# Hybrid encoder block on one core: values' stores on another queue, key halves written by the engines, other pages behind the last gates

## Chip, cores and metric

One Trainium2 chip, one core of it. The metric is the device time of one execution of the whole program in microseconds; lower is better. All arithmetic is fp32: an fp32 product is made of three matmuls on a rounded part ("high", written by ScalarE as a copy to the matmul's fp32r type) and the rest of the number ("low", written by VectorE as a subtraction).

## Reference

One layer of a streaming encoder on x (512 tokens, width 2048):

```python
h = rms_norm(x, norm_mix_w)
q_a, k_a, v_a, q_g, k_g, v_g, r_g, gate_lr = split_cols(h @ w_in, IN_SPLITS)
y_a = chunked_band_attention(q_a, k_a, v_a, att_rel_bias)       # 16 heads of 64, chunks of 64 frames, 8 chunks back
o_g = gated_linear_attention(q_g, k_g, v_g, log_a)              # 4 heads, keys 128, values 256 wide
y_g = rms_norm(o_g, gla_norm_w) * silu(r_g)
x = x + concat(y_a, y_g) @ w_out
h = rms_norm(x, norm_ffn_w)
u_gate, u_val = split(causal_depthwise_conv(h @ w_ffn_up, w_ffn_conv, b_ffn_conv))
x = x + (gelu(u_gate) * u_val) @ w_ffn_down
g = sigmoid(rms_norm(x, norm_ple_w) @ w_ple_gate)
x = x + g * (p @ w_ple_proj)                                    # per-layer embedding p, 256 wide
return rms_norm(x, final_norm_w)
```

In the attention, scores are `q·k / 8 + bias`, a softmax over the keys of the band, and the weighted sum of the values.

## The kernel before

Activations are kept transposed: 128 rows of features by 512 tokens. The program runs in this order: the values of the gated linear attention, its four heads, the values of the softmax attention (`values_a(0)`, then `values_a(1)`, each for 8 of the 16 heads), then a list of *steps*.

**Values.** `values_a(c)` calls `vproj`, which accumulates four PSUM tiles `ps[t]` (one for 128 tokens), and ScalarE copies them, scaled, into four half pages (`vstage`). Four DMAs on SyncE's queue then store them to the scratch tensor `vad` in DRAM (L1018). Each attention unit later loads its 128 columns back as `va` (L710). Before `vproj` of `c = 1` copies its results, it calls `operands_left`, which issues eight loads of operands of the input stage (`in_N`, `in_T`, `in_R`, L337).

**Steps.** The other matrix products are done in the form of a seven-product block scheme. A *unit* is a pair of 128-row output blocks; it takes seven steps P1, P2, P6, P5, P7, P3, P4, each of 24 matmuls of 128x256 for a full-length product. The stages, in order: `pp` (embedding products, units 0 and 1, one step `PP` each), `in` (12 units: 0 to 7 queries and keys of one pair of heads each, 8 to 11 the gates `r_g`), `pp` (units 2 and 3), `wo` (output projection, 8 units, its first two interleaved step by step), `up`, three `dn` stages, `pg`.

The loop over the steps writes the order of the engines by hand: for step *i* it emits ScalarE's high part and VectorE's low part of the weights of step *i*+2, the step's matmuls, and what an *agenda* holds for this step, sorted by a small number (below 2 ahead of the product, from 2 on behind it); then `collect` takes the finished product from PSUM into the unit's page `unit.o`, named `u` in the profile. For VectorE, ScalarE and TensorE the program order is kept in this part; DMAs on the queues of SyncE, ScalarE and GpSimd are placed by the compiler's scheduler.

**Pages.** 128x1024 fp32 buffers have fixed tags, and `page(ring, name)` hands them out in turn from a ring of tags. At first ring `c` is only (`c0`) and ring `u` is (`u0`, `u1`); after the last attention unit (`attention_done`) `c` is (`c1`, `c2`, `c0`) and `u` is (`u2`, `u3`, `u0`, `u1`). A page that is handed out again is written only when its earlier readers, stores among them, are done.

After the switch ring `c` gives, in this order: `on` of gates 1 and 2 (`after_gates`, the attention's result that a gate multiplies), `pT` (the embedding's input), `on` of gate 3, two `pp_o` pages of embedding unit 2, two of unit 3, then `xs` of the `wo` units. Ring `u` gives `u2` and `u3` to gates 2 and 3, and `u0`, `u1` to the first two units of `wo`.

**Embedding.** `embedding(unit)` makes four products into PSUM (`pp`), ScalarE copies them into two `pp_o` pages, and after each second copy a DMA on ScalarE's queue stores the page to `ppd` (L687).

**Attention.** `attend(unit)` returns agenda items relative to the end of the unit's products, so that the attention of a pair of heads runs beside the products of the next unit. For each of the two heads `s` of a pair, the query page holds the high part of Q in one half of the partitions and the low part in the other, and the key pages `Kh` and `Kl` must hold the same 64 rows twice, once in each half, so that one matmul gives high plus low. `high` (ScalarE, second step) writes Q's high part and one half of `Kh`; `low` (VectorE, third step) writes Q's low part into the other half and one half of `Kl`; `double` (third step) copies each half to the other with four DMAs on GpSimd's queue. `scores` (from the fifth step on) multiplies into `psc`, `soft`, `normal`, `turn`, `evict` and `values` follow.

GpSimd's queue also carries the weight loads that add in place (`accum_op`, L404), which make the sums of weight blocks that the scheme needs.

Of the kernel before, what the change touches and what calls it, by code (L numbers as in the profile page):

```python
# [8 lines left out]
F32 = mybir.dt.float32  # L9
F32R = mybir.dt.float32r  # L10
I32 = mybir.dt.int32
AF = mybir.ActivationFunctionType
ALU = mybir.AluOpType

P = 128
# [26 lines left out]
def encoder_block(ctx: ExitStack, tc: tile.TileContext, A, out):  # L42
    nc = tc.nc
# [4 lines left out]
    pg = ctx.enter_context(tc.tile_pool(name="pages", bufs=1))  # L48
# [21 lines left out]
    vec, act, ten = InOrder(nc.vector), InOrder(nc.scalar), InOrder(nc.tensor)  # L70
# [26 lines left out]
    def page(ring, name, dt=F32, shape=(P, 1024)):  # L97
        tags = rings[ring]
        i = counts.get(ring, 0)
        counts[ring] = i + 1  # L100
        tag = tags[i % len(tags)]
        return page_pool(tag).tile(list(shape), dt, tag=tag, name=name)
# [562 lines left out]
    vad, ond = scratch("vad", (8, P, TT, P)), scratch("ond", (4, P, 2, T))  # L665
    ps_, early = [], []
# [6 lines left out]
    def embedding(unit):  # L673

        hi, lo = unit.w["PP"]
        for i in range(4):
            if i % 2 == 0:
                o = (early[0].tile([P, 1024], F32, tag="pp_o", name="pp_o", bufs=4) if unit.u < 2 else page("c", "pp_o"))
                o = o.rearrange("p (s t) -> p s t", s=2)
            pp = psum_aux("pp")  # L680
            for k in range(2):
                w = slice((i * 2 + k) * P, (i * 2 + k + 1) * P)
                product3(pp, hi[:, w], lo[:, w], ps_[0][:, k], k == 0, k == 1)
            act.activation(o[:, i % 2, :], pp, AF.Copy)
            if i % 2:
                m = 4 * unit.u + i - 1
                nc.scalar.dma_start(ppd[m % 8:m % 8 + 2, m // 8].rearrange("m p t -> p m t"), o)  # L687
# [6 lines left out]
    def attend(unit):  # L694
        b, M = unit.u, {}
        o = unit.o

        def tile_(name, cols, dt=F32, tag=None, bufs=1):
            return att[0].tile([P, cols], dt, tag=tag or name, name=name, bufs=bufs)

        def load_e():
            for s in range(2):
                nc.sync.dma_start(bias[:, s, :], A["bias"][2 * b + s])

        def mask():
            vec.memset(bias[0:64, :, T - CHUNK:T], NEG)

        def load_v():
            M["V"] = tile_("va", T).rearrange("p (k v) -> p k v", k=TT)
            nc.sync.dma_start(M["V"], vad[b])  # L710

        def high():
            for n in ("Q", "Kh", "Kl"):
                for s in range(2):
                    M[n, s] = tile_(f"{n}{s}", T, F32R)
            for s in range(2):
                a = slice(s * 64, s * 64 + 64)
                act.activation(M["Q", s][a], o[a, 0, :], AF.Copy, scale=0.125)
                act.activation(M["Kh", s][a], o[a, 1, :], AF.Copy)

        def low():
            for s in range(2):
                a, z = slice(s * 64, s * 64 + 64), slice(64 - s * 64, 128 - s * 64)
                vec.scalar_tensor_tensor(M["Q", s][z], o[a, 0, :], 0.125, M["Q", s][a].bitcast(F32), ALU.mult, ALU.subtract)
                vec.tensor_tensor(M["Kl", s][a], o[a, 1, :], M["Kh", s][a].bitcast(F32), ALU.subtract)

        def double():
            for s in range(2):
                a, z = slice(s * 64, s * 64 + 64), slice(64 - s * 64, 128 - s * 64)
                for n in ("Kh", "Kl"):  # L730
                    nc.gpsimd.dma_start(M[n, s][z], M[n, s][a])

        def scores(h):
            for s in range(2):
                psc = M["psc", s, h] = psum_aux("psc")
                for i, qt in enumerate(TILES[h]):
                    w = slice(256 * i, 256 * i + max(P * (qt + 1), 256))
                    nn = w.stop - w.start
                    ql = M["Q", s][:, qt * P:(qt + 1) * P]
                    ten.matmul(psc[:, w], ql, M["Kh", s][:, :nn], start=True, stop=False)  # L740
                    ten.matmul(psc[:, w], ql, M["Kl", s][:, :nn], start=False, stop=True)

        def soft(h):
            t, at = tile_("sc", 1024, bufs=2), 0
            for s in range(2):
                for i, qt in enumerate(TILES[h]):
                    n = P * (qt + 1)
                    sc = M["sc", s, qt] = t[:, at:at + n]
                    mx = M["mx", s, qt] = tile_("mx", 4, bufs=8)
                    at += n  # L750
                    vec.tensor_tensor_reduce(sc, M["psc", s, h][:, 256 * i:256 * i + n], bias[:, s, T - n:T], 1.0, -3.0e38,
                                             ALU.add, ALU.max, mx[:, 0:1])
                    vec.tensor_scalar(mx[:, 1:2], mx[:, 0:1], -1.0, None, ALU.mult)
                    act.activation(sc, sc, AF.Exp, bias=mx[:, 1:2], accum_out=mx[:, 2:3])

        def normal(h):
            for s in range(2):
                for qt in TILES[h]:
                    sc, mx = M["sc", s, qt], M["mx", s, qt]
                    vec.reciprocal(mx[:, 3:4], mx[:, 2:3])  # L760
                    vec.tensor_scalar(sc, sc, mx[:, 3:4], None, ALU.mult)

        def turn(h):
            for s in range(2):
                ptr = M["ptr", s] = psum_aux("ptr")
                for i, qt in enumerate(TILES[h]):
                    for kt in range(qt + 1):
                        ten.transpose(ptr[:, (2 * i + kt) * P:(2 * i + kt + 1) * P], M["sc", s, qt][:, kt * P:(kt + 1) * P], ident)

        def evict(h):  # L770
            n = 3 * P if h else T
            M["PT"] = tile_("PT", 2 * T).rearrange("p (s t) -> p s t", s=2)
            for s in range(2):
                act.activation(M["PT"][:, s, :n], M["ptr", s][:, :n], AF.Copy)

        def values(h):
            if h == 0:
                M["y"] = pp_.tile([P, T], F32, tag="b3", name="py")
            for i, qt in enumerate(TILES[h]):
                for kt in range(qt + 1):  # L780
                    for s in range(2):
                        o = (2 * i + kt) * P
                        ten.matmul(M["y"][s * 64:(s + 1) * 64, qt * P:(qt + 1) * P], M["V"][:, kt, s * 64:(s + 1) * 64],
                                   M["PT"][:, s, o:o + P], start=kt == 0, stop=kt == qt)

        def result():
            if b % 2 == 0:
                ypair[:] = [page("c", "yp").rearrange("p (s t) -> p s t", s=2)]
            act.activation(ypair[0][:, b % 2, :], M["y"], AF.Copy)

        items = [(2, 0, load_e), (2, 2, high), (3, 1, low), (3, 3, double), (4, 1, mask), (5, 0, load_v), (11, 1, result)]
        if b % 2:
            items.append((12, 1, lambda: store_pair(mixd, b // 2, ypair[0][:, 0, :], ypair[0][:, 1, :])))
        for h in range(3):
            items += [(t + h, k, lambda f=f, h=h: f(h)) for t, k, f in (
                (5, 6, scores), (6, 1, soft), (7, 1, normal), (7, 5, turn), (8, 1, evict), (8, 4, values))]
        return items
# [54 lines left out]
    agenda = [[] for _ in range(len(steps) + 60)]  # L852
    now = [0]
    for a, b in zip(stages[3:], stages[4:]):
        i0 = base[a.units[-1]]
# [12 lines left out]
    i0 = base[front.units[-1]]  # L868
# [12 lines left out]
    def embedding_load(raw):  # L881
        nc.sync.dma_start(raw.rearrange("p (k t) -> p k t", k=2), A["p"].rearrange("k p t -> p k t"))
        return raw
# [4 lines left out]
        vec.tensor_tensor(t[:, 1, :], raw, t[:, 0, :].bitcast(F32), ALU.subtract)  # L888

    raws = {}  # L890
    agenda[i0 + 2].append((0, lambda: raws.update(p=embedding_load(page("c", "pT")))))
    agenda[i0 + 6].append((1, lambda: embedding_split(raws["p"], xtile("N1", 1, "ps"))))

    def attention_done():
# [116 lines left out]
    def values_a(c, between=None, then=None):  # L1011
        def place(t):
            vstage[c, t] = xslot(4 * c + t, "va")
            return vstage[c, t]

        vproj(A["w_v_a"], c, place, between=between, then=then)
        for t in range(TT):
            nc.sync.dma_start(vad[4 * c:4 * c + 4, :, t].rearrange("b p v -> p b v"),  # L1018
                              vstage[c, t].rearrange("p (b v) -> p b v", b=4))

    shim = ctx.enter_context(tc.tile_pool(name="shim", bufs=1, side="right")).tile([P, 240], F32, tag="shim", name="shim")
# [213 lines left out]
    for i, (unit, prod) in enumerate(steps[:-4]):  # L1235
# [19 lines left out]
        if i - len(steps) in EARLY:  # L1255
            p, op, g = EARLY[i - len(steps)]
# [160 lines left out]
```

## Time and profile before

| | |
|---|---|
| median of 3 runs | 2329.81 us (2325.82 to 2332.3) |
| profiled execution, device time | 2329.97 us |
| its span, first to last instruction | 2328.3 us |
| mean granted TensorE clock | 0.99 |
| busy in the span: PE, DVE, ACT, POOL | 2273.8, 1879.8, 1287.6, 161.1 us |
| DMA | 520.84 MB, mean 224 GB/s |
| 300 to 317 us | end of the second values product |
| 317 to 329 us | first embedding products |
| 329 to 650 us | input stage, from 372 us on with the attention beside it |
| 650 to 663 us | second embedding products |
| from 663 us | output projection, then the feed-forward stages |

Rows of a timeline give start, length, engine, line, operation, `out<-in` by the program's names, the count of merged instructions, and in brackets how long the engine had idled before and what ended that. "ACTq" and "SPq" are the queues of ScalarE and SyncE when they issue a DMA. Rows of a table by stretches give the stretch, its length, the busy time and instruction count of PE, PEld, DVE, ACT and POOL, the granted clock, the share of the DMA engines and GB/s. Most code of the steps goes through one helper and so has line L64; the tile names tell the operations apart.

### The profile page before, as it was taken

How to read it: one execution, taken by the hardware profiler on the slowest of the kernel's cores; microseconds unless marked ns; L12 is line 12 of the kernel's file. 1: busy time of each engine (PE TensorE's matmuls, PEld its weight loads, DVE VectorE, ACT ScalarE, POOL GpSimd, SP SyncE). 2: the span in 40 equal slices, each digit the busy share in tenths (PEclk: the TensorE clock that was granted, in tenths of full speed). 3: DMA queues.
4: the chain of work that ended last, by engine and by line, in shares of the span. 5: the costliest groups of instructions: out<-in, count | busy, mean ns of one | idle time of the engine just before them, and what ended most of it. 6: DMA issues, size and time to landing. Idle time of an engine off the chain costs nothing.

```text
span 2328.3 us, 44943 instructions
## 1 busy us (share of the span) xinstructions
PE 2273.8 (98%) x17980; PEld 2190.4 (94%) x17980; DVE 1879.8 (81%) x2557; ACT 1287.6 (55%) x1878; POOL 161.1 (7%) x212
## 2 busy tenths in 40 slices
PE   9999999999999999999999999999999999999996
PEld 8878879999989999999999999999999999999995
DVE  6556357888788898998888888888898787898987
ACT  6344355666565565555555555555564554656655
POOL 0000001111000010000000100000000100001000
PEclk9999999999999999999999999999999999999998
DMA  6622577777897987788777777777866967879894
GB/s 217 195 77 89 174 265 182 194 197 198 262 303 242 298 237 210 209 221 219 215 210 218 208 219 209 210 218 210 254 211 228 317 223 237 274 254 329 264 293 158
DMA packets 198033, 520.84 MB, mean 224 GB/s; under 512 B 21408, under 2 KB 72864, under 8 KB 197824
## 3 DMA queue, kind: packets, MB, share of 16 engines
q1 hardware_dynamic: 167296, 422.54, 52.2%
q0 software_dynamic: 26176, 89.14, 21.4%
q10 hardware_dynamic: 4352, 6.29, 0.7%
q8 instruction: 141, 2.31, 0.4%
q14 instruction: 68, 0.56, 0.1%
HBM read 435.05 MB, written 76.55 MB: 220 GB/s over the span
## 4 chain that ended last, share of the span: by engine, by line
PE 82%; DVE 7%; DMA 6%; ACT 3%; issue 2%; SPq 0%; POOL 0%; ACTq 0%; DVEq 0%; POOLq 0%
PE accA L64 38%; PE accC L64 19%; PE accB L64 10%; PE v L249 3%; PE v L251 2%; PE v L250 2%; DVE wl L64 2%; DMA Kl<-Kl 1%; DMA s<-in_w_blk 1%; DVE s L64 1%; DMA s<-in_w_dn 1%; DVE u L64 1%; PE pk L133 1%; PE pk L132 1%; PE pk L134 1%
## 5 line engine op out<-in xcount | busy, mean ns | idle before, releaser
L64 DVE TENSOR_TENSOR wl<-s,wh 128x1024 fp32r<-128x1024 f32 (+1 forms) x365 | 437.8, 1200 | 67.4 <-ACT wh L64 66.5
L64 DVE TENSOR_TENSOR wl<-l,wh 128x1024 fp32r<-128x1024 f32 (+1 forms) x308 | 368.5, 1196 | 73.3 <-ACT wh L64 72.6
L64 ACT ACTIVATE wh<-l 128x1024 fp32r<-128x1024 f32 (+1 forms) x308 | 319.2, 1037 | 182.5 <-PE accC L64 120.0
L64 ACT ACTIVATE wh<-s 128x1024 fp32r<-128x1024 f32 (+1 forms) x365 | 378.0, 1037 | 36.0 <-DVE s L64 16.6
L64 ACT ACTIVATE u<-accA 128x256 f32<-128x256 f32 x290 | 110.0, 379 | 378.0 <-PE accA L64 377.5
L64 DVE TENSOR_TENSOR s<-s,l 128x1024 f32<-128x1024 f32 (+1 forms) x192 | 229.7, 1196 | 8.7 <-DMA s<-in_w_blk 8.7
L64 PE MATMUL accA<-up_T,wh 128*128 128x256 f32 x1408 | 178.7, 279 | 0.1
L64 PEld LDWEIGHTS accA<-up_T,wh 128*128 128x128 f32 x1408 | 170.5, 188 | 0.3 <-ACT wh L64 0.3
L64 DVE SCALAR_TENSOR_TENSOR cv<-u,cw,cv 128x511 f32<-128x511 f32 (+1 forms) x176 | 131.6, 748 | 3.1
L404 POOL DMA_DIRECT2D s<-in_w_up x88 | 75.1, 853 | 790.3 <-DMA s<-in_w_up 363.3
L249 PE MATMUL v<-wv_h,h 128*128 128x512 f32 x256 | 100.2, 391 | 0.6 <-ACT h L154 0.6
L250 PE MATMUL v<-wv_l,h 128*128 128x512 f32 x256 | 100.4, 392 | 0.0
L251 PE MATMUL v<-wv_h,h 128*128 128x512 f32 x256 | 99.9, 391 | 0.0
L64 PE MATMUL accA<-up_T,wl 128*128 128x256 f32 x704 | 96.3, 279 | 0.0
L64 PE MATMUL accA<-dn_T,wh 128*128 128x256 f32 x704 | 91.3, 282 | 4.2 <-ACT wh L64 4.2
L64 ACT ACTIVATE u<-accC 128x256 f32<-128x256 f32 x94 | 36.0, 383 | 106.6 <-PE accC L64 106.5
L64 PE MATMUL accB<-up_R,wh 128*128 128x256 f32 x704 | 90.4, 280 | 2.0 <-DVE up_R L64 1.3
L64 PEld LDWEIGHTS accA<-dn_T,wh 128*128 128x128 f32 x704 | 86.5, 190 | 4.8 <-ACT wh L64 4.8
L64 PE MATMUL accA<-up_R,wh 128*128 128x256 f32 x704 | 89.6, 279 | 0.0
L64 PE MATMUL accC<-up_R,wh 128*128 128x256 f32 x704 | 89.2, 279 | 0.0
L64 PE MATMUL accA<-up_N,wh 128*128 128x256 f32 x704 | 89.2, 279 | 0.0
L64 PE MATMUL accC<-up_N,wh 128*128 128x256 f32 x704 | 89.2, 279 | 0.0
(388 smaller groups left out, 5126.7 us busy)
## 6 DMA issues: line engine op xcount, KB each, us to landing
l<-in_w_up SPq DMA_DIRECT2D x132, 512.0 KB, 5.3
s<-in_w_up SPq DMA_DIRECT2D x88, 512.0 KB, 4.8
s<-in_w_up POOLq DMA_DIRECT2D x88, 512.0 KB, 6.2
l<-in_w_dn SPq DMA_DIRECT2D x56, 448.0 KB, 5.2
l<-in_w_blk SPq DMA_DIRECT2D x36, 512.0 KB, 4.9
l<-in_w_out SPq DMA_DIRECT2D x28, 512.0 KB, 5.2
l<-in_w_dn SPq DMA_DIRECT2D x28, 512.0 KB, 5.4
s<-in_w_blk SPq DMA_DIRECT2D x24, 512.0 KB, 5.1
```

Of the source, the lines that this page charges most:

```text
L64: ins = f(*args, **kw)
L132: nc.tensor.matmul(po, whi, act[:, 0, :], start=start, stop=False)
L133: nc.tensor.matmul(po, whi, act[:, 1, :], start=False, stop=False)
L134: nc.tensor.matmul(po, wlo, act[:, 0, :], start=False, stop=stop)
L249: nc.tensor.matmul(ps[t], h1[kt][:, 0, sl], wh, start=kt == 0, stop=False)
L250: nc.tensor.matmul(ps[t], h1[kt][:, 0, sl], wl, start=False, stop=False)
L251: nc.tensor.matmul(ps[t], h1[kt][:, 1, sl], wh, start=False, stop=kt == KD - 1)
L404: nc.gpsimd.dma_start(t, src("L22" if name == "S1" else "L11"), accum_op=ALU.add)
```

## The change

1. The four stores of the values of `c = 1` are issued on ScalarE's queue; those of `c = 0` stay on SyncE's.
2. `high` and `low` write both halves of `Kh` and `Kl`, two more instructions on ScalarE and two more on VectorE for a pair of heads; `double` and its four GpSimd DMAs are gone.
3. `pT` takes page `u0`, and the first `pp_o` of embedding unit 3 takes page `u1`; both no longer draw from ring `c`. So `on` of gate 3 has `c0`, unit 2 has `c1` and `c2`, unit 3 has `u1` and `c0`, and the first `xs` pages have `c1`, `c2`, `c0`.

```diff
-                o = (early[0].tile([P, 1024], F32, tag="pp_o", name="pp_o", bufs=4) if unit.u < 2 else page("c", "pp_o"))
+                o = (early[0].tile([P, 1024], F32, tag="pp_o", name="pp_o", bufs=4) if unit.u < 2 else
+                     pg.tile([P, 1024], F32, tag="u1", name="pp_o") if (unit.u, i) == (3, 0) else page("c", "pp_o"))
...
                 act.activation(M["Q", s][a], o[a, 0, :], AF.Copy, scale=0.125)
-                act.activation(M["Kh", s][a], o[a, 1, :], AF.Copy)
+                for r in (a, slice(64 - s * 64, 128 - s * 64)):
+                    act.activation(M["Kh", s][r], o[a, 1, :], AF.Copy)
...
-                vec.tensor_tensor(M["Kl", s][a], o[a, 1, :], M["Kh", s][a].bitcast(F32), ALU.subtract)
-
-        def double():
-            for s in range(2):
-                a, z = slice(s * 64, s * 64 + 64), slice(64 - s * 64, 128 - s * 64)
-                for n in ("Kh", "Kl"):
-                    nc.gpsimd.dma_start(M[n, s][z], M[n, s][a])
+                for r in (a, z):
+                    vec.tensor_tensor(M["Kl", s][r], o[a, 1, :], M["Kh", s][a].bitcast(F32), ALU.subtract)
...
-        items = [(2, 0, load_e), (2, 2, high), (3, 1, low), (3, 3, double), (4, 1, mask), (5, 0, load_v), (11, 1, result)]
+        items = [(2, 0, load_e), (2, 2, high), (3, 1, low), (4, 1, mask), (5, 0, load_v), (11, 1, result)]
...
-    agenda[i0 + 2].append((0, lambda: raws.update(p=embedding_load(page("c", "pT")))))
+    agenda[i0 + 2].append((0, lambda: raws.update(p=embedding_load(pg.tile([P, 1024], F32, tag="u0", name="pT")))))
...
-            nc.sync.dma_start(vad[4 * c:4 * c + 4, :, t].rearrange("b p v -> p b v"),
+            (nc.scalar if c else nc.sync).dma_start(vad[4 * c:4 * c + 4, :, t].rearrange("b p v -> p b v"),
                               vstage[c, t].rearrange("p (b v) -> p b v", b=4))
```

## The prediction

> **What bounds the kernel now.** I read the page first, then PE's busy time by stretches, then who PE waited for, then the timelines round those waits. The page says that PE is busy nearly all the time, so a gain must come out of places where PE stands still.
>
> ```profile
> PE 2273.8 (98%) x17980; PEld 2190.4 (94%) x17980; DVE 1879.8 (81%) x2557; ACT 1287.6 (55%) x1878; POOL 161.1 (7%) x212
> ```
>
> Between 700 and 2000 us PE misses 5.4 of 1300 us, so whatever the stages before save or lose there passes unchanged to the end:
>
> ```profile
> 700.00:2000.00 1300.00, 1294.57 (x11064) 1291.77 (x11064) 1120.69 (x1322) 710.15 (x972) 98.16 (x115) 1.00 0.79 231
> ```
>
> All edits lie between 315 and 690 us. PE's waits in 300 to 700 us (total, times, longest):
>
> ```profile
> PE psc L64 <- DMA Kl<-Kl: 5.8, 3, 3.4
> PE accA L64 <- ACT u L64: 5.6, 2, 4.1
> PE accA L64 <- DVE wl L64: 2.4, 2, 1.3
> PE pp L64 <- DVE ps L64: 1.1, 1, 1.1
> ```
>
> The first row is the copy of the low key half by GpSimd's DMA, the second mostly one wait of 4.1 us at the start of the input stage, the last two lie at the second round of embedding products. A stall also costs what the clock loses behind it:
>
> ```profile
> 339.10:344.39 5.29, 5.29 (x25) 5.29 (x26) 5.29 (x7) 2.79 (x3) 0.00 (x0) 0.50 0.41 142
> 344.39:347.19 2.80, 2.80 (x24) 2.80 (x24) 2.28 (x2) 1.33 (x2) 0.00 (x0) 0.95 0.67 215
> 521.54 0.50 PE L64 MATMUL psc<-Kl,Q 128*128 128x512 f32 x1 [1.67 <-DMA Kl<-Kl]
> 521.50:524.70 3.20, 3.16 (x26) 3.12 (x27) 2.62 (x8) 1.63 (x4) 0.00 (x0) 1.00 0.68 195
> 2142.94 2.05 PE L64 MATMUL accB<-pg_R,wh 128*128 128x256 f32 x8 [2.23 <-ACT pg_R L64]
> 2143.00:2145.00 2.00, 1.99 (x8) 1.56 (x8) 2.00 (x4) 2.00 (x7) 0.00 (x0) 0.62 1.09 310
> ```
>
> After the stall of 4.1 us one product of 24 matmuls took 5.29 us at a granted clock of 0.50, the next 2.80: the low clock cost 2.49. After a gap of 1.67 the clock stayed at 1.00; after one of 2.23 it was 0.62. So I count the surcharge for gaps over about 2 us.
>
> **Part A, the values' stores.** Here is the 4.1 us wait: first ScalarE, then SyncE's queue, then PE, then a piece of the chain that ended last, then a row of SyncE's waits:
>
> ```profile
> 329.91 1.09 ACT L64 ACTIVATE pp_o<-pp 128x512 f32<-128x512 f32 x2 [0.44 <-ACT pp_o L64]
> 334.47 0.37 ACTq L687 DMA_DIRECT2D ppd<-pp_o  x1
> 334.88 2.00 ACT L64 ACTIVATE in_R<-in_R 128x1024 fp32r<-128x1024 f32 x2 [3.89 <-DMA ppd<-pp_o]
> ...
> 338.69 0.36 ACT L64 ACTIVATE u<-accA 128x256 f32<-128x256 f32 x1
> ```
>
> ```profile
> 319.06 1.37 SPq L337 DMA_DIRECT2D in_R<-h_R  x2
> 324.39 0.37 SPq L1018 DMA_DIRECT2D vad<-pair_u  x1
> 330.95 0.37 SPq L1018 DMA_DIRECT2D vad<-pair_c  x1
> ```
>
> ```profile
> 333.87 1.09 PE L64 MATMUL accB<-in_R,wl 128*128 128x256 f32 x8
> 339.10 1.22 PE L64 MATMUL accA<-in_N,wh 128*128 128x256 f32 x4 [4.13 <-ACT u L64]
> ```
>
> ```profile
> 325.13 9.27 DMA ppd<-pp_o
> ```
>
> ```profile
> SPq L1018 <- DMA ppd<-pp_o: 6.1, 1, 6.1
> ```
>
> ScalarE finished its last embedding eviction at 331.00 (329.91 + 1.09), but its fourth store was issued only at 334.47, just after the second one (issued 325.13, 9.27 us on the way) had landed. That store reads another buffer, and SyncE's store of values at 330.95 likewise waited for a ScalarE store that it has nothing to do with. I read this as a limit on the DMAs of the two queues in flight, taken in turn: the fourth embedding store waits for the DMA some eight places before it. Two of the places between are the third and fourth stores of values, issued late, at 324.39 and 330.95. On ScalarE's queue all four follow their evictions, ahead of the first embedding store, so the DMA eight places back becomes an `in_R` load of 319.06, landed by about 328.3 even if it took 9.27 us (estimate). The 3.47 us block (331.00 to 334.47) goes.
>
> What comes last then? The same ScalarE work, 3.47 us earlier: PE could start at 335.63 (339.10 - 3.47); it is ready at 334.96 (333.87 + 1.09). Against this stand four issues more on ScalarE, 0.37 each, 1.48 in all; behind them on that engine are the weight split and the embedding evictions, and PE waits for those through its banks. Fully absorbed, PE starts at 335.63 (stall 0.67), not at all, at 337.11 (2.15). I take the middle, 336.4, a stall of 1.4 that keeps the clock, being nearer to the 1.67 than to the 2.23 row: 2.7 earlier plus 2.49 of clock, **5.2 us**. Ends: 6.6 (4.13 + 2.49), and a loss of 1.5, if the issues push an eviction that PE waits for and the block stays. SyncE's queue, freed of a store that waited 6.1 us, can send its weights and bias earlier; nothing waits for them there, so I count nothing.
>
> [...]
>
> **Part B, the key halves.** From one head pair's first score matmul to the next one's, seven periods, the first and the one in which PE never waited:
>
> ```profile
> 372.52:406.20 33.68, 30.28 (x246) 28.79 (x245) 22.97 (x57) 18.33 (x39) 4.75 (x7) 0.90 0.66 166
> ...
> 491.44:519.01 27.57, 27.57 (x247) 26.49 (x245) 22.94 (x58) 18.28 (x39) 3.94 (x6) 1.00 0.75 202
> ...
> sum 203.71, PE 196.87 PEld 187.23 DVE 163.64 ACT 128.70 POOL 28.40; mean PE 28.12 PEld 26.75 DVE 23.38 ACT 18.39 POOL 4.06
> ```
>
> Seven times 27.57 is 193.0; the sum is 203.7: the periods lose **10.7 us** to the late key copy, 6.1 of it in the first (a 3.4 us wait and the low clock behind it). Out go four GpSimd DMAs for each of eight pairs; GpSimd is 7% busy, so its own time is worth nothing. In come two more ScalarE and two more VectorE instructions a pair, priced by their twins:
>
> ```profile
> L64 DVE TENSOR_TENSOR Kl<-u,Kh 64x512 fp32r<-64x512 f32 x16 | 11.0, 686 | 0.5
> L64 ACT ACTIVATE Kh<-u 64x512 fp32r<-64x512 f32 x16 | 9.8, 616 | 0.0
> ```
>
> 1.37 us of VectorE and 1.23 of ScalarE a pair. Their cover, in one pair:
>
> ```profile
> 510.24 0.69 DVE L64 TENSOR_TENSOR Kl<-u,Kh 64x512 fp32r<-64x512 f32 x1
> 513.97 1.23 DVE L64 TENSOR_TENSOR wl<-l,wh 128x1024 fp32r<-128x1024 f32 x1 [1.65 <-ACT wh L64]
> 509.57 0.85 ACT L64 ACTIVATE PT<-ptr 128x384 f32<-128x384 f32 x2
> 512.50 0.88 PE L64 MATMUL py<-PT,va 128*64 128x128 f32 x12
> ```
>
> VectorE ends its halves at 510.93, then at 512.30, and idles 1.65 us soon after, which takes the 1.37. ScalarE's next eviction for PE ends at 510.42, then at 511.65, and PE reads it at 512.50: 0.85 to spare. The scores come 8 us after 510.93 (519.01), so the halves are early. I take 0.5 off for small new waits: **10.2 us**. Ends: 10.7, and a loss of 10.1, if all 2.60 us of all eight pairs fell on PE's path (20.8 against 10.7).
>
> **Part C, pages behind the last gates.** At the second embedding round ScalarE waits for a page whose store has not landed:
>
> ```profile
> 662.04 0.37 ACTq L687 DMA_DIRECT2D ppd<-pp_o  x1
> 664.01 1.09 ACT L64 ACTIVATE pp_o<-pp 128x512 f32<-128x512 f32 x2 [2.00 <-DMA ppd<-pp_o]
> 666.64 1.83 DVE L64 TENSOR_TENSOR wo_T<-wo_T 128x1024 fp32r<-128x1024 f32 x2 [2.63 <-ACT wo_T L64]
> 673.36 0.37 ACT L64 ACTIVATE u<-accA 128x256 f32<-128x256 f32 x1
> DMA to landing us min/median/max: 6.6/8.7/9.3
> ```
>
> With four different pages, free long before, the 2.00 goes. Behind it VectorE had idled for ScalarE's `wo_T` split, and later PE waits 2.4 us for VectorE. But the `wo_T` data itself, loaded shortly before, may come next; I take **1.0**, between 0 and 2.0. The new hold is page `u1`: the write at 673.36 (the second `u` of the output stage) must now wait for the store issued at 662.04, at the slowest landed by 671.3. Even 2.00 earlier ScalarE reaches it at 671.36; a loss would need a landing over 11.3 us. Page `u0` under the embedding input changes no order on ScalarE or VectorE, so the 1.1 us wait for `ps` stays.
>
> **Sum.** 5.2 + 10.2 + 1.0 = 16.4 us. The profiled execution took 2329.97, 1.67 more than its span and 0.16 above the median of 2329.81, so I take it from the median: 2313.4, said as **2313.5**. All good ends: 19.3, 2310.5; all bad ends: 11.6 slower, 2341.4.
>
> **Rivals.**
> 1. The move of the stores buys nothing: ScalarE only pays 1.5 us, because a store now blocks it for its place among the DMAs in flight, as the store at 334.47 does. 10.2 + 1.0 - 1.5 = 9.7: 2320. For it: the in-order blocking is real, and where the compiler puts the four issues isn't known. Against: ScalarE's own evictions gate the stores, so they are among the first in turn. Chance 0.15. [...]
> 2. Other late data takes the copy's place before the scores (weights, with a DMA share of 0.66 and 0.75 in the two rows above): B halves to 5. Total 11.2: 2318.6. Against: the period at 491.44 shows 27.57 with the same loads. Chance 0.12.
> 3. Slower: the added halves make ScalarE and VectorE the late engines. If their 2.60 us a pair outran the cover of 1.65 and 0.85 and PE stalled by all of it, each stall is over the 2.23 at which the clock fell: 8 x (2.60 + 2.49) = 40.7, less 10.7, less 6.2 for A and C: 23.8 slower, 2353.6. It decides from more than about 2 us of lateness a pair. Against: the scores come 8 us later. Chance 0.06.
> 4. The change doesn't do what it says: the blocks come from the order of other DMAs and stay, the scores wait for something else that ends at the same time. 2327 to 2330. Chance 0.05.
>
> **How the numbers follow.** My case has 0.62. With rivals 1 and 2 that is 0.89 for a gain; a measurement here tells about 0.3% (7 us) from no change, and I leave 0.02 of it for gains under that: faster 0.87, same 0.07, slower 0.06. The range runs from 2309 (all good ends and the runs' scatter) to 2325 (rivals 1 and 2 with scatter), leaving out 3 and 4 and tails.
>
> **What would show it.** Right: no wait of PE's score matmuls for `Kl`; periods near 27.6; the first `accA<-in_N` about 336.4 on the old scale at a clock near 1.00; four value stores on ScalarE's queue before the first embedding store; no 2.00 us wait at the third `pp_o`. Wrong: ScalarE idle for a DMA between 316 and 335; PE waiting for `wl` or `PT` in the periods; a wait of `u` for an embedding store.

## The result, and the profile after

The changed kernel takes 2316.57 us (median of 5 runs, 2311.97 to 2323.15) against 2329.81 (5 runs, 2325.82 to 2332.3): 13.2 us less, a ratio of 0.9946 with a 95% interval of 0.9929 to 0.9964. It was forecast at 2313.5, 16.3 less. The profiled execution was the longest of the five (2323.15, span 2321.4), so the places of the gains are read from the trace and the total from the runs.

The engines' row of the page, then PE's waits between 300 and 700 us (total, times, longest):

```profile
PE 2279.7 (98%) x17980; PEld 2198.5 (95%) x17980; DVE 1892.2 (82%) x2573; ACT 1295.6 (56%) x1894; POOL 143.1 (6%) x180
```

```profile
PE accA L64 <- DVE wl L64: 2.4, 2, 1.3
PE accB L64 <- DVE wl L64: 1.5, 3, 0.8
PE accA L64 <- ACT u L64: 1.5, 1, 1.5
PE pp L64 <- DVE ps L64: 1.1, 1, 1.1
PE pp L64 <- ACT pair_c L255: 1.0, 1, 1.0
```

The row of the key copy (5.8 us) is gone and the wait for `u` has lost its 4.1. The waits for `wl` behind the second embedding round are the same 2.4 and 0.8 as before.

**Part A.** ScalarE's timeline, then SyncE's queue, PE, and the stretch of 3.30 us in which the first product behind the old wait runs:

```profile
318.27 0.54 ACTq L1015 DMA_DIRECT2D vad<-pair_c  x1
...
329.52 1.09 ACT L64 ACTIVATE pp_o<-pp 128x512 f32<-128x512 f32 x2 [0.44 <-ACT pp_o L64]
330.63 0.37 ACTq L688 DMA_DIRECT2D ppd<-pp_o  x1
331.05 2.01 ACT L64 ACTIVATE in_R<-in_R 128x1024 fp32r<-128x1024 f32 x2 [0.44 <-ACT pp_o L64]
```

```profile
309.10 0.95 SPq L337 DMA_DIRECT2D in_N<-h_N  x2
```

```profile
335.27 2.16 PE L64 MATMUL accA<-in_N,wh 128*128 128x256 f32 x16
...
338.20 2.05 PE L64 MATMUL accC<-in_N,wh 128*128 128x256 f32 x16
```

```profile
335.27:338.57 3.30, 3.30 (x29) 3.30 (x29) 3.30 (x4) 2.96 (x4) 0.00 (x0) 1.00 0.49 193
```

The fourth embedding store is issued the moment its eviction ends, `in_R` follows 0.44 us later instead of 3.89, and PE has no wait at `accA<-in_N` that the timeline marks. That product starts at 335.27 instead of 339.10, keeps clock 1.00, and the next starts at 338.20 instead of 344.39: 6.2 us earlier.

**Part B.** The seven periods, the first, the second and the sum:

```profile
367.13:395.20 28.07, 28.07 (x247) 26.53 (x245) 24.67 (x60) 19.28 (x41) 1.70 (x2) 1.00 0.74 181
395.20:422.77 27.57, 27.57 (x246) 26.49 (x245) 25.00 (x63) 19.42 (x41) 1.70 (x2) 1.00 0.69 183
...
sum 193.51, PE 193.51 PEld 185.48 DVE 172.69 ACT 135.79 POOL 11.93; mean PE 27.64 PEld 26.50 DVE 24.67 ACT 19.40 POOL 1.70
```

203.71 has become 193.51: 10.2 us. VectorE and ScalarE are busier in each period (24.67 for 23.38 and 19.40 for 18.39 on average) and PE is never idle.

**Part C.** ScalarE at the third embedding store of the second round:

```profile
648.24 0.37 ACTq L688 DMA_DIRECT2D ppd<-pp_o  x1
648.65 1.09 ACT L64 ACTIVATE pp_o<-pp 128x512 f32<-128x512 f32 x2 [2.04 <-DMA wo_T<-mix_T]
```

The 2.00 us wait for a page is now a wait of 2.04 at the same eviction, released by another transfer.

**The way down the span.** Starts of the same instruction, before and after: the second product behind the wait 344.39 and 338.20 (6.2 gained), the first scores 372.52 and 367.13 (5.4, so 0.8 had been given back, about half of it at a wait for `wl`), the end of the seventh period 576.23 and 560.64 (15.6), the output stage 700.29 and 684.91 (15.4). From there on the two traces should run in parallel, and they don't:

```profile
900.00:1700.00 800.00, 800.00 (x6859) 800.00 (x6858) 698.17 (x828) 431.80 (x584) 68.47 (x81) 1.00 0.79 218
```

```profile
900.00:1700.00 800.00, 800.00 (x6795) 800.00 (x6794) 695.21 (x821) 426.50 (x575) 68.26 (x80) 1.00 0.79 218
```

The first is the kernel before, the second the changed one. Both show PE busy all the time at full granted clock, yet the changed one did 64 matmuls less: 117.7 ns each instead of 116.6, which costs 7.5 us in this stretch. The change touches nothing there; this is taken up after the experiments.

### The profile page after: what moved, and what is told of

Its sections match the earlier page's. It is cut to its first block, busy times and chain, and to the rows that moved or that the text cites. A ratio compares the mean times of both kernels' runs of the same rounds, so it can differ in the third digit from the quotient of the medians.

```text
span 2321.4 us, 44878 instructions
## 1 busy us (share of the span) xinstructions
PE 2279.7 (98%) x17980; PEld 2198.5 (95%) x17980; DVE 1892.2 (82%) x2573; ACT 1295.6 (56%) x1894; POOL 143.1 (6%) x180
## 4 chain that ended last, share of the span: by engine, by line
PE 88%; DVE 5%; DMA 3%; ACT 2%; issue 1%; SPq 0%; ACTq 0%; DVEq 0%
PE accA L64 40%; PE accC L64 21%; PE accB L64 10%; PE v L249 2%; PE v L251 2%; PE v L250 2%; DVE wl L64 1%; PE py L64 1%; PE psc L64 1%; PE ptr L64 1%; DVE s L64 1%; PE pk L133 1%; PE pk L132 1%; PE pk L134 1%; PE pq L134 1%
## 5 line engine op out<-in xcount | busy, mean ns | idle before, releaser
L64 DVE TENSOR_TENSOR s<-s,l 128x1024 f32<-128x1024 f32 (+1 forms) x192 | 230.0, 1198 | 11.3 <-DMA s<-in_w_blk 11.3
L64 PEld LDWEIGHTS accB<-up_R,wh 128*128 128x128 f32 x704 | 87.1, 190 | 2.7 <-DVE up_R L64 1.5
```

Source lines behind the costliest of these rows:

```text
L64: ins = f(*args, **kw)
```

## The experiments

The letters are the change's parts. "At 700 us" means the start of the same matmul in the trace of before, minus that in the experiment's.

### Each part alone, and the change again

`e1_stores` is before with part A alone:

```diff
-            nc.sync.dma_start(vad[4 * c:4 * c + 4, :, t].rearrange("b p v -> p b v"),
+            (nc.scalar if c else nc.sync).dma_start(vad[4 * c:4 * c + 4, :, t].rearrange("b p v -> p b v"),
```

> The kernel before with the values' stores of c = 1 on ScalarE's queue, nothing else. My theory (part A is independent of the rest): the wait of 4.1 us before the first accA<-in_N goes, that product starts near 335.3 as in the changed kernel and runs at full clock, 6.3 us earlier by the next product; the waits for the key copies stay, so the whole is 5 to 6.5 us faster, about 2324. Rival (the stores alone only save issue time, the stage was freed by the other edits): the wait stays and the time is within 1.5 us of before.

Measured: 2327.75 against 2332.07, ratio 0.9985 (0.9967 to 1.0003), which does not exclude no change at all. In its trace 6.5 us are gained between the first embedding product and the second product behind the old wait, but the first wait for the key copy, 3.40 before, has grown:

```profile
374.78 0.79 PE L64 MATMUL psc<-Kl,Q 128*128 128x512 f32 x1 [4.82 <-DMA Kl<-Kl]
```

PE comes earlier and the copy does not follow in step, so 1.4 us of A are handed back at the next late transfer. At 700 us this trace is 7.3 ahead.

`e2_keys` is before with part B alone:

```diff
-                act.activation(M["Kh", s][a], o[a, 1, :], AF.Copy)
+                for r in (a, slice(64 - s * 64, 128 - s * 64)):
+                    act.activation(M["Kh", s][r], o[a, 1, :], AF.Copy)
...
-                    nc.gpsimd.dma_start(M[n, s][z], M[n, s][a])
+                for r in (a, z):
+                    vec.tensor_tensor(M["Kl", s][r], o[a, 1, :], M["Kh", s][a].bitcast(F32), ALU.subtract)
```

> The kernel before with both key halves written by ScalarE and VectorE, nothing else. My theory: the 4.1 us wait stays, every period between the heads' first score matmuls is 27.6 us, 10.2 to 10.7 us in all, about 2319.5. Rival (weights' landing or the engines come last instead): periods stay above 28, the gain is 5 us or less.

Measured: 2323.38, ratio 0.9962 (0.9946 to 0.9977). Over the seven periods its trace gains 10.7 us, the whole of what they lost; the wait for `u` stays.

`e3_pages` is before with part C alone:

```diff
-                o = (early[0].tile([P, 1024], F32, tag="pp_o", name="pp_o", bufs=4) if unit.u < 2 else page("c", "pp_o"))
+                o = (early[0].tile([P, 1024], F32, tag="pp_o", name="pp_o", bufs=4) if unit.u < 2 else
+                     pg.tile([P, 1024], F32, tag="u1", name="pp_o") if (unit.u, i) == (3, 0) else page("c", "pp_o"))
...
-    agenda[i0 + 2].append((0, lambda: raws.update(p=embedding_load(page("c", "pT")))))
+    agenda[i0 + 2].append((0, lambda: raws.update(p=embedding_load(pg.tile([P, 1024], F32, tag="u0", name="pT")))))
```

> The kernel before with the other pages for pT and the first pp_o of embedding unit 3, nothing else. My theory after the result: the 2.0 us wait of ScalarE for a page turns into a wait of about the same length at the third embedding store, for its place among the DMAs in flight, and nothing is gained: within 0.5 us of before on the path at 700 us. Rival (the prediction's part C): 1 us earlier at the first accC<-wo_N.

Measured: 2334.71, ratio 1.001 (0.9993 to 1.0028): no gain, and 0.4 us behind at 700 us. ScalarE's timeline:

```profile
663.83 0.37 ACTq L688 DMA_DIRECT2D ppd<-pp_o  x1
664.24 1.09 ACT L64 ACTIVATE pp_o<-pp 128x512 f32<-128x512 f32 x2 [3.14 <-DMA wo_T<-mix_T]
```

With pages to spare ScalarE now stands before the *issue* of the third store, until a load of the output stage has landed: the fourth store of part A over again.

`e4_again` is the changed kernel once more, beside these three.

> The changed kernel once more, beside the others. My theory: the program is 15.4 us ahead at 700 us in every execution, and what is missing of it at the end is the spacing of the matmuls between 820 and 2130 us, which changes from execution to execution (117.8 against 116.7 ns) and not with the edits: this profile may show either spacing, and the runs spread over some 10 us. Rival: the slow spacing belongs to the changed program, and every profile with the key halves shows it.

Measured: 2320.61 against 2332.07, ratio 0.9946 (0.9927 to 0.9966), the same ratio; 17.4 us at 700 us, 0.6 of it already gained at the first embedding product, ahead of every edit. The three parts' medians alone come to -4.3, -8.7 and +2.6, together -10.4; the change as a whole gives -11.5.

### What part A took away: two stores at a time

`e5_late_two` and `e6_early_two` move only half of the four stores:

```diff
-            nc.sync.dma_start(vad[...]
+            (nc.scalar if c and t > 1 else nc.sync).dma_start(vad[...]      # e5_late_two
+            (nc.scalar if c and t < 2 else nc.sync).dma_start(vad[...]      # e6_early_two
```

> The kernel before with only the third and fourth stores of the values of c = 1 on ScalarE's queue; the first and second stay on SyncE's, ahead of the in_N loads. It splits part A: SyncE's queue head is still held by the first stores until their evictions end, so the in_N loads are still issued late (about 315 us), but no late store takes a place in the turn of the DMAs. Theory (the turn): the fourth embedding store is issued without a wait, ScalarE's 3.9 us before in_R goes, the first accA<-in_N starts about 335 to 337 and the clock holds; 4 to 6 us less at 372 us, 3 to 6 us less in the time. Rival (the late in_N loads held by SyncE's queue are the cause): the wait of about 4 us stays, 0 to 1 us.

> The kernel before with only the first and second stores of the values of c = 1 on ScalarE's queue; the third and fourth stay on SyncE's, behind the loads of the input stage's operands. The other half of part A: SyncE's queue is free for the in_N loads about 7 us earlier, but two stores of values stand late on it. Theory (the turn): they still take places between the embedding stores, so ScalarE still waits 2 to 4 us for the fourth embedding store; 0 to 2 us less. Rival (the head of SyncE's queue): the wait is gone, accA<-in_N starts at 335 to 337, 4 to 6 us less.

Measured: 2326.04 (ratio 0.9973, 0.9945 to 1.0002) and 2329.93 (0.9999, 0.9979 to 1.0019) against 2328.67; the runs don't settle it, the traces do. ScalarE, PE and the stretch behind the wait, late two first, then early two:

```profile
331.47 0.37 ACTq L687 DMA_DIRECT2D ppd<-pp_o  x1
331.88 1.08 ACT L64 ACTIVATE pp_o<-pp 128x512 f32<-128x512 f32 x2 [2.08 <-DMA ppd<-pp_o]
```

```profile
337.63 2.15 PE L64 MATMUL accA<-in_N,wh 128*128 128x256 f32 x16 [2.58 <-ACT u L64]
```

```profile
337.62:340.92 3.30, 3.29 (x28) 3.30 (x29) 3.30 (x4) 2.97 (x4) 0.00 (x0) 1.00 0.81 313
```

```profile
330.48 0.37 ACTq L687 DMA_DIRECT2D ppd<-pp_o  x1
330.89 1.09 ACT L64 ACTIVATE pp_o<-pp 128x512 f32<-128x512 f32 x2 [2.29 <-DMA ppd<-pp_o]
```

```profile
336.99 2.14 PE L64 MATMUL accA<-in_N,wh 128*128 128x256 f32 x16 [2.19 <-ACT u L64]
```

```profile
336.98:340.28 3.30, 3.29 (x28) 3.29 (x29) 3.30 (x4) 2.98 (x4) 0.00 (x0) 1.00 0.11 43
```

Neither theory holds as it was put. With either half the block moves from the fourth store to the third and is shorter: PE's wait of 4.13 becomes 2.58 or 2.19, and behind both the granted clock is 1.00. From the first embedding product to the second product behind the wait the traces gain 3.9 and 4.3, of the 6.5 that all four stores gave: 2.4 of the clock, and 1.5 and 1.9 of the wait's 4.1. The turn itself stays the prediction's reading; the traces show the times that go with it. In before the fourth embedding store goes out at 334.47, 0.07 us behind the second's landing at 334.40 (325.13 + 9.27). In both kernels here ScalarE stands still at the third store, 2.08 and 2.29 us, until an embedding store has landed (the brackets above). In the changed kernel, with all four stores ahead, the `in_R` loads go out at 320.28 and 321.06 and have landed by 325.4 (4.4 us at the slowest), and the fourth embedding store goes out at 330.63, 0.02 us behind its eviction (329.52 + 1.09).

### What part B took away: `Kl` alone

`e7_kl_only` lets VectorE write both halves of `Kl`; `Kh` is still doubled by GpSimd's DMAs, and ScalarE gets nothing more to do.

```diff
-                vec.tensor_tensor(M["Kl", s][a], o[a, 1, :], M["Kh", s][a].bitcast(F32), ALU.subtract)
+                for r in (a, z):
+                    vec.tensor_tensor(M["Kl", s][r], o[a, 1, :], M["Kh", s][a].bitcast(F32), ALU.subtract)
...
-                for n in ("Kh", "Kl"):
+                for n in ("Kh",):
```

> The kernel before, VectorE writes both halves of Kl, and Kh is still copied by GpSimd's DMAs (two for a pair instead of four); nothing is added to ScalarE. Theory (only Kl's copies were late, being the last of four on GpSimd's queue and written last): all seven periods near 27.6, no wait of the scores for a key page, 9.5 to 11 us less at 576 us, as with both halves. Rival (Kh's copies come next): a wait of the scores for Kh of 0.5 to 2 us in the first period, 28 and more, 5 to 8 us less.

Measured: 2323.48, ratio 0.9966 (0.9943 to 0.999), as B alone within the intervals. Six periods fall to 27.57, but the first only to 30.6, and not for `Kh`: its trace gains 7.6 in the periods where B alone gains 10.7. GpSimd's queue in B alone, then in this kernel; SyncE's two plain weight loads with their time to landing, in B alone and in this kernel; then this kernel's VectorE and PE:

```profile
367.29 0.85 POOL L404 DMA_DIRECT2D s<-in_w_blk  x1 [15.53 <-ACT u L64]
369.07 0.86 POOL L404 DMA_DIRECT2D s<-in_w_blk  x1 [0.93 <-DMA s<-in_w_blk]
```

```profile
363.98 0.52 POOL L732 DMA_DIRECT2D Kh<-Kh  x1 [0.63 <-ACT Kh L64]
369.33 0.90 POOL L404 DMA_DIRECT2D s<-in_w_blk  x1 [4.82 <-DVE wl L64]
371.31 0.86 POOL L404 DMA_DIRECT2D s<-in_w_blk  x1 [1.08 <-DVE u L64]
```

```profile
362.56 1.46 SPq L403 DMA_DIRECT2D s<-in_w_blk  x2
DMA to landing us min/median/max: 4.1/4.5/4.8
```

```profile
362.65 1.46 SPq L403 DMA_DIRECT2D s<-in_w_blk  x2
DMA to landing us min/median/max: 6.0/6.5/6.9
```

```profile
377.30 1.23 DVE L64 TENSOR_TENSOR s<-s,l 128x1024 f32<-128x1024 f32 x1 [4.62 <-DMA s<-in_w_blk]
```

```profile
381.92 0.33 PE L64 MATMUL ptr<-ident,sc 128*128 128x128 f32 x1 [2.46 <-DVE sc L64]
```

GpSimd also issues the adding weight loads. With the `Kh` copies they go out at 369.33 and 371.31, without any at 367.29 and 369.07. They do not queue behind the copies: the second copy is issued by 364.50 (363.98 + 0.52), and the queue then stands idle for 4.82 us. Each adding load needs the plain load of the same page to have landed. SyncE issues the plain loads at the same time in both kernels, but they take 6.0 and 6.9 us while the copies are on the way, 4.1 and 4.8 without: landed at 368.69 and 370.72 instead of 366.65 and 368.51, each about 0.6 us ahead of the adding load's issue. (The brackets of the adding loads name the engine that signalled last, not this landing.) VectorE's next sum, which reads the page, then starts at 377.30 instead of 372.89: it has waited 4.62 us (0.30 in B alone) in front of the scores' softmax, and PE waits 2.46 for the result. The same shows, weaker, over the whole attention part: between 335 and 575 us these plain loads took 3.4 to 7.6 us, 5.1 in the median, in before, with the copies, and 3.5 to 6.2, 4.5 in the median, in the changed kernel, without. So in the first period B was worth 6.1 for two reasons of about the same size: the late key copy, and the weight loads that the copies slowed.

### What stood behind part C

`e8_pp_gpsimd` is the changed kernel with the stores that block ScalarE put on GpSimd's queue:

```diff
-                nc.scalar.dma_start(ppd[m % 8:m % 8 + 2, m // 8].rearrange("m p t -> p m t"), o)
+                (nc.scalar if unit.u < 2 else nc.gpsimd).dma_start(ppd[m % 8:m % 8 + 2, m // 8].rearrange("m p t -> p m t"), o)
```

> The changed kernel with the four embedding stores of units 2 and 3 on GpSimd's queue instead of ScalarE's, so that ScalarE doesn't stand behind a store that waits for its place in the turn. Theory (C's gain went into the wait at the third store's issue): ScalarE's wait of 2.0 us at the third pp_o goes, VectorE's wait for ScalarE's wo_T shrinks, and PE's waits for wl between 655 and 668 us (3.2 us in all) shrink by 0.8 to 1.5; 0 to 1.5 us less than the changed kernel in the trace between 640 and 690 us. Rival (the landing of the wo_T data, about 648 to 649 us, comes last whatever ScalarE does): PE's waits there stay within 0.3 us.

Measured: 2318.9 against 2328.67, ratio 0.9942 (0.992 to 0.9965), not told apart from the change. ScalarE's wait at the third store goes, and with it PE's three waits for `wl` (3.2 us with the one for `accB`). GpSimd's queue, ScalarE and PE:

```profile
652.50 1.79 POOL L688 DMA_DIRECT2D ppd<-pp_o  x2
```

```profile
661.13 0.38 ACT L64 ACTIVATE u<-accA 128x256 f32<-128x256 f32 x1 [4.46 <-DMA ppd<-pp_o]
```

```profile
662.51 3.79 PE L64 MATMUL accA<-wo_N,wh 128*128 128x256 f32 x16 [3.07 <-ACT wh L64]
```

Between 640 and 690 us the trace loses 1.5 us against the changed kernel's. The last stores wait in GpSimd's queue behind a weight load and go out at 652.50; now the page `u1` is held, ScalarE waits 4.46 for it, PE 3.07, and the granted clock behind that is 0.50 (662.00 to 668.00). This is the hold that the prediction named for `u1`, here brought about by a late issue.

`e9_u1_first` is that kernel with `u1` given to unit 2's first pair, whose store goes early:

```diff
-                     pg.tile([P, 1024], F32, tag="u1", name="pp_o") if (unit.u, i) == (3, 0) else page("c", "pp_o"))
+                     pg.tile([P, 1024], F32, tag="u1", name="pp_o") if (unit.u, i) == (2, 0) else page("c", "pp_o"))
```

> The run before it with the stores of embedding units 2 and 3 on GpSimd's queue, and page u1 given to unit 2's first pair instead of unit 3's, so that the late store on GpSimd's queue no longer holds the page of the second u of the output stage (units: u1, c1, then c2, c0). Theory (part C's 2 us on ScalarE are worth what they were priced at once no store stands in front of ScalarE and no late page behind it): ScalarE waits neither for its place at a store nor for u, PE's waits for wl (0.80, 1.27, 1.08 in the changed kernel) and the 3.07 for wh both go; 2.5 to 3.3 us less than the changed kernel between 640 and 690 us, 0 to 4 us less in the time (the scatter of the later stages is as large). Rival (the last output weights or the xs load come next): one of the waits stays or an equal one comes, less than 1 us gained.

Measured: 2314.44 against 2325.21, ratio 0.995 (0.9934 to 0.9967). The wait for `u` is gone too, and the rival comes true. SyncE's queue, ScalarE and PE:

```profile
654.50 0.38 SPq L533 DMA_DIRECT2D xs<-in_x  x1
654.97 1.48 SPq L337 DMA_DIRECT2D wo_N<-mix_N  x1
```

```profile
663.30 0.63 ACT L64 ACTIVATE wo_N<-wo_N 128x512 fp32r<-128x512 f32 x1 [6.23 <-DMA wo_N<-mix_N]
```

```profile
665.55 2.97 PE L64 MATMUL accA<-wo_N,wh 128*128 128x256 f32 x16 [2.92 <-ACT wh L64]
```

The `wo_N` load goes out at 654.97, behind an `xs` load at the head of SyncE's queue; in the changed kernel it went out at 652.93. It lands last, and ScalarE waits 6.23 us for it, 3.09 in the changed kernel. Between 640 and 690 us the trace loses 1.2 us against the changed kernel's.

`e10_no_pages` is the changed kernel without part C (C's lines put back as before).

```diff
-                o = (early[0].tile([P, 1024], F32, tag="pp_o", name="pp_o", bufs=4) if unit.u < 2 else
-                     pg.tile([P, 1024], F32, tag="u1", name="pp_o") if (unit.u, i) == (3, 0) else page("c", "pp_o"))
+                o = (early[0].tile([P, 1024], F32, tag="pp_o", name="pp_o", bufs=4) if unit.u < 2 else page("c", "pp_o"))
...
-    agenda[i0 + 2].append((0, lambda: raws.update(p=embedding_load(pg.tile([P, 1024], F32, tag="u0", name="pT")))))
+    agenda[i0 + 2].append((0, lambda: raws.update(p=embedding_load(page("c", "pT")))))
```

> The changed kernel without part C: stores and key halves as changed, pT and pp_o pages from ring c as before. Theory (C bought nothing, the wait only changed its name): ScalarE waits 2 to 3 us before its third pp_o, PE's waits for wl stay at 3 us or 1 us over, the time within 1.5 us of the changed kernel's (about 0.9945 of before). Rival (C is worth its 1.0 to 2.0 us): the trace loses 1 to 2 us against the changed kernel between 640 and 690 us.

Measured: 2315.92 against 2325.21, ratio 0.9957 (0.994 to 0.9973). ScalarE:

```profile
645.88 1.09 ACT L64 ACTIVATE pp_o<-pp 128x512 f32<-128x512 f32 x2 [1.71 <-DMA ppd<-pp_o]
```

The old wait is back at 1.71 and PE's waits behind it are the same three. Without C nothing is lost that these runs can tell. The traces even speak against C: at 700 us this one is 18.1 ahead of before's, the change's 15.4 and its repeat's 17.4. From 576 to 700 us all five traces with C lose against before's (0.2 to 3.3 us; the most in `e8_pp_gpsimd` and `e9_u1_first`, which have other edits there), and all seven others without C gain on it (0.7 to 2.1). A part of that lies at one wait of PE for ScalarE's `u`, 1.45 us in the change and 0.37 here, but 1.46 in before. In the change `pT` is loaded early, at 575.83, ahead of the weight loads that are issued next; whether that costs the time is not shown, and each run has one trace.

`e11_stores_kl` is before with part A and `Kl` alone of part B (the edits of `e1_stores` and `e7_kl_only` together).

> The kernel before with the stores of values of c = 1 on ScalarE and both halves of Kl by VectorE; Kh still doubled by GpSimd's DMAs (two a pair), pages as before. Theory (a Kh copy is in time only by a margin, and the stores on ScalarE start the first scores 5.4 us earlier while the copies queue behind the weight sums on GpSimd): the first period shows a wait of the scores for Kh of 0.5 to 4 us that the kernel with Kl alone did not show, the other six are near 27.6; 10 to 15 us less at 700 us. Rival (Kh's copies have room): seven periods near 27.57, 15 to 16 us less at 700 us, and the time equal to the changed kernel's without any more work on ScalarE.

Measured: 2313.8 against 2325.21, ratio 0.995 (0.9931 to 0.9968); 14.5 us at 700 us. The wait of the first period is there, but for the softmax, as in `e7_kl_only` (VectorE waits 4.16 us for the sum), not for `Kh`:

```profile
376.64 1.25 PE L64 MATMUL ptr<-ident,sc 128*128 128x128 f32 x8 [2.68 <-DVE sc L64]
```

Half of B's new instructions give most of B; the rest is 2.7 us of PE's time in one period. No version beats the changed kernel by more than the intervals.

## Why the prediction came out right, point by point

- **The place.** All that was gained lies between 317 and 577 us, as forecast, and it came down the span through the output stage unchanged (15.6 at 576, 15.4 at 700).
- **Part A, 5.2 forecast, 6.2 in the trace.** What the reading foretold came: the `in_R` loads have landed by 325.4, and the fourth store goes out 0.02 us behind its eviction. The count of some eight places stays an estimate from the order of the issues: the times show the hold and its end, not the count. The mis-sized term is the middle of 1.4 us for the four added issues: PE starts at 335.27 without a stall, earlier even than the 335.63 of "fully absorbed", so their 1.48 us cost nothing. The term that was missing is that 0.8 of it is given back before the first scores.
- **"SyncE's queue, freed ... so I count nothing".** The `in_N` loads went out 7.85 us earlier (309.10 for 316.95). That this was worth anything by itself is not shown: `e5_late_two` gained 3.9 us with these loads as late as before (316.50), `e6_early_two` 4.3 with them early (308.61), and each move also changes which DMAs go out ahead of the embedding stores.
- **Part B, 10.2 forecast, 10.2 measured,** without any wait of PE for `wl` or `PT` in the periods; the covers of 1.65 and 0.85 held. The cause was only half of it: the prediction laid all 10.7 us to the late key copy. GpSimd's own time is indeed worth nothing, but its copies slowed the weight loads that were on the way beside them, which `e7_kl_only` prices at some 3 of the first period's 6.1. That forecast and measurement agree to a tenth is luck: the 0.5 taken off for new waits is met by 0.5 us in the first period of this profile (28.07), and B alone lost none of it (193.0 for seven periods; the repeat 193.3).
- **Part C, 1.0 forecast, nothing measured,** and by the traces rather a loss. The step that failed is "with four different pages ... the 2.00 goes". It named the data behind it (`wo_T`) but not the place: the third store of this round is held until another DMA has landed, as part A's fourth store was in before (3.14 us with C alone, 2.04 in the change). Where that is taken away, two more holds follow, 4.46 for `u1` and 6.23 for `wo_N`. The margin given for `u1` was wrong too: with ScalarE 2.00 us earlier, as the same sentence has it, a landing over 9.3 us (671.36 - 662.04) would do, not 11.3, and the slowest store took 9.3. The hold did not come in the change, where that store landed after 8.5 us.
- **Rival 1** is refuted: no store of values blocks ScalarE. The move was worth more than the issues that it shifted: ScalarE had stood 3.47 us before an issue of 0.37, and 4.13 us of PE's wait and 2.49 us of the low clock behind it went. **Rival 2** came true only in the first period of `e7_kl_only` and `e11_stores_kl`, **rival 3** nowhere. **Rival 4**, that the blocks come from the order of other DMAs and stay, is what happened to part C.
- **The total, 16.4 forecast, 13.2 in the medians.** Up to 700 us the trace lost nothing of the parts but C: 5.4 of A at the first scores, 10.2 of B and 0.2 lost behind them make 15.4, and the repeat has 17.4. The rest, 2 to 6 us, is not the parts' doing as far as the traces show; it lies in the spacing of matmuls and in single stalls after 700 us.

**The spacing of matmuls, open.** Of the 13 profiles six show 6851 to 6860 matmuls between 900 and 1700 us, seven 6794 or 6795: before has 6859, part A alone 6794, `e6_early_two` 6860, `e5_late_two` 6795, the change and its repeat 6795, without C 6851. No edit sorts them: `e9_u1_first` and `e10_no_pages` have parts A and B like the change, and the narrow spacing. All 13 traces hold the same 17980 matmuls in the same order, so the difference is not one of missing records. The spacing changes within an execution. In the change's profile the wide one lasts from about 886 to past 2100 us, and its lead over before falls from 15.4 us at 820 to 4.9 at 2000; the runs of one kernel lie about as far apart (2322.64 to 2338.68 in 30 runs of before). What sets it, and whether the change alters its odds, wasn't settled, and with it neither were the last 2 to 6 us.

## What to carry to other kernels

A DMA that waits at the head of a queue costs what is queued behind it, here 3.47 us of ScalarE's time: look, for each issue that is late, at the DMA that released it, even one of another queue and another buffer, and move away the stores that stand between the two and become ready late. Removing DMAs can be worth as much for the loads that were on the way beside them as for themselves: in the first period some 3 of 6.1 us. Before a wait for a buffer is priced as a gain, find the next hold at the same instruction; here there were four in a row, and the stage behind them started no earlier.

## What the runs showed of the hardware

- **Two steady rhythms at full granted clock.** The same 128x256 matmuls, back to back, come every 116.6 or every 117.7 ns (800 us divided by 6859 and by 6795) for hundreds of microseconds, both at a granted clock of 1.00.
- **A gap's length alone does not tell the clock behind it.** After 2.58 us in `e5_late_two` and 2.19 in `e6_early_two` the clock stayed at 1.00 (the rows above), where the prediction counted a surcharge from about 2 us on, from the 0.62 behind 2.23 in before. Yet in `e8_pp_gpsimd` two short gaps in a row were enough:

```profile
597.57 1.20 PE L64 MATMUL accB<-in_R,wl 128*128 128x256 f32 x8 [0.44 <-DVE wl L64]
600.22 3.63 PE L64 MATMUL accA<-in_N,wh 128*128 128x256 f32 x16 [1.46 <-ACT u L64]
```

```profile
600.22:603.20 2.98, 2.98 (x14) 2.98 (x15) 2.91 (x6) 1.84 (x2) 0.00 (x0) 0.53 0.85 291
```

  In `e9_u1_first` gaps of 1.75 and 1.45 at the same place left it at 1.00 (600.97 to 603.90). Even two like gaps ahead of the same instructions can differ, as in stage `up`, in before and then in the changed kernel:

```profile
831.41 1.47 PE L64 MATMUL accB<-up_R,wh 128*128 128x256 f32 x8 [0.76 <-ACT up_R L64]
834.15 1.06 PE L64 MATMUL accB<-up_R,wh 128*128 128x256 f32 x4 [1.26 <-DVE up_R L64]
836.00:838.00 2.00, 2.00 (x20) 2.00 (x19) 2.00 (x3) 0.73 (x1) 0.00 (x0) 1.00 0.60 121
```

```profile
816.03 1.47 PE L64 MATMUL accB<-up_R,wh 128*128 128x256 f32 x8 [0.77 <-ACT up_R L64]
818.77 1.25 PE L64 MATMUL accB<-up_R,wh 128*128 128x256 f32 x4 [1.27 <-DVE up_R L64]
820.00:822.00 2.00, 2.00 (x12) 2.00 (x11) 2.00 (x4) 0.11 (x1) 0.00 (x0) 0.50 0.95 209
```

  What sets these apart is not shown. The gaps over 3 us whose clock was read here were all followed by a lower one: 3.07 in `e8_pp_gpsimd` (0.50 from 662.00 to 664.00), and in before 3.12 (0.56 from 2016.73 to 2020.60), 3.40 (0.50 from 376.78 to 382.20) and 4.13 (0.50 from 339.10 to 344.39). For the shorter ones a forecast can only give the loss of the clock a chance.
